# Moving one gate block's weight halves ahead of a plane copy and two turned halves in a two-branch attention kernel

## The chip, the cores and the metric

The kernel runs on one core of a Trainium2 chip. The metric is the device time of one execution in microseconds. Before the change the median of three runs is 749.95 us (749.94 to 751.45). The core has a matrix engine (PE, with its weight loads as PEld), three engines for the rest (DVE, the vector engine; ACT, the scalar engine; POOL, called GpSimd), and SyncE (SP), which here only issues DMAs. Each engine works through its own instructions in the order of the program; between engines there are only semaphore waits.

## The reference, cut to what matters

One layer over 512 frames of width 1024: two attention branches and their gates from one projection, a merge, an output projection, LayerNorm, a gated MLP with a short causal convolution, LayerNorm. Branch A (`dsa`) selects 128 keys per query by top-k over an indexer's scores and then attends with 8 heads of 64; branch B (`sb`) is stick-breaking attention, also 8 heads of 64.

```python
def sb_sequence(q, k, v):                      # per head and block of 128 queries
        causal = s_pos[None, :] < t[:, None]
        z = jnp.einsum('thd,shd->hts', qb, k).astype(jnp.float32) * HEAD_DIM ** -0.5
        log_beta = jax.nn.log_sigmoid(z)
        log_keep = jnp.where(causal, jax.nn.log_sigmoid(-z), 0.0)
        later = lax.cumsum(log_keep, axis=2, reverse=True) - log_keep
        a = jnp.where(causal, jnp.exp(log_beta + later), 0.0).astype(v.dtype)
        return jnp.einsum('hts,shd->thd', a, v)
...
        proj = x @ w_in[layer]
        q_a, k_a, v_a, q_i, k_i, w_i, q_s, k_s, v_s, g_a, g_b = jnp.split(proj, IN_OFFSETS, axis=-1)
...
        y_a = lax.map(lambda a: dsa_sequence(*a, rel_bias),
...
        y_s = lax.map(lambda a: sb_sequence(*a),
...
        gate_a = jax.nn.sigmoid(g_a + b_gates[layer, 0])
        gate_b = jax.nn.sigmoid(g_b + b_gates[layer, 1])
        merged = gate_a * (y_a @ w_branch_dsa[layer]) + gate_b * (y_s @ w_branch_sb[layer])
        x = layer_norm(DEEPNORM_ALPHA * x + merged @ w_out[layer], ln1_g[layer], ln1_b[layer])
        u, g = jnp.split(x @ w_ffn_in[layer], 2, axis=-1)
        h = jax.nn.gelu(causal_dwconv(u, conv_w[layer], conv_b[layer])) * g
        x = layer_norm(DEEPNORM_ALPHA * x + h @ w_ffn_out[layer], ln2_g[layer], ln2_b[layer])
```

## The kernel before, in words

**Arithmetic.** Every f32 operand of a matmul is split into a high half and a low half (rest), each in the matrix engine's fp32r format, and a product is made of three matmuls: high by high, low by high, high by low. In the code the halves of the activations are `xh`, `xl`, those of the weights `whi`, `wlo`. A projection block (`proj_t`, L234 to L236) is 24 matmuls of 512 columns: 8 slices of the width, three products each, into one PSUM bank.

**Weights** stream through `Stream`: a DMA brings a 128x1024 block into `raw` (ring of three), ACT makes the high half `whi` (L105), and the low half `wlo` is made either by DVE or POOL as `raw - whi` (L114) or, for some blocks (the gates gb4 to gb7 among them), by ACT as `-whi` (L108) and a DMA that adds the block from DRAM to it (L111). `asp` says how many blocks ahead the stream splits, `behind` behind which instruction the next high half is tied, `highs` keeps the instruction of L108. The blocks come in a fixed list; around the change it is qa0, ka0, gb4, gb5, gb6, gb7, qa1, ka1, va: the gates of branch B, queries and keys of branch A, its values.

**Heads of branch B.** For one head the scores `z` (L536, PSUM `z_ps`) go through two sigmoids on ACT (L541 `keep`, L542 `beta`), scans on DVE and a product on POOL. The weights are then turned: `send_planes` splits them in two 16-bit planes (L472 on ACT for the high plane `keep<-beta`, L473 on POOL for the low plane) and issues one DMA transpose for each on SP into the single buffer `pl`; `join_planes` puts the planes together again (L483 on ACT, L484 on POOL, into `back`) and splits the result in fp32r halves `pth` (L486, ACT, "turned half") and `ptl` (L491, DVE). `weigh` (L507) multiplies them with the values into `av_ps`, ACT takes one half out (L512, `avt`).

**Around the change** heads 4, 5, 6 and 7 of branch B are under way, one being weighed while the next is turned and the one behind it is scored. Between them stand fillers: gate blocks, then qa1 (copied out by ACT at L357), ka0 and ka1, each taken out of its PSUM bank by `stack_hl` as two ACT copies (L339, L340) and two DVE subtractions (L341, L342), then the values `va` (`proj_v`, L271 to L273), whose four accumulators `va_ps0` to `va_ps3` take the four banks of the same PSUM pool that gb6, gb7, qa1 and ka1 had. DVE also does the rounds of the top-k selection (L424, L425). Behind them the heads of branch A start: logits `l_ps` (L581), masked by DVE (L587, `lg`), exponential on ACT (L590).

**The order.** The program is written in Tile with a scheduler that works out each engine's order from its own estimate of times; the code ties one instruction behind another with `tc.issue_after`. Before the change, head 5's planes are sent as soon as head 5's scans are done (in `advance`), head 4's turned halves follow in `join_planes(..., first=True)`, gb6's high half is tied behind head 4's turned half, and ka0's copies behind gb6's L108. The rounds of selection of turn 4 are tied behind head 4's low half.

Of the kernel before, what the change touches and what calls it, by code (L numbers as in the profile page):

```python
# [49 lines left out]
def r32(ap):  # L50
    return ap.bitcast(F32)
# [77 lines left out]
def tile_block(ctx: ExitStack, tc: tile.TileContext, xT, xN, w_qi, w_ki, w_t, w_v, w_br, w_o, w_fi, w_fo,  # L129
# [305 lines left out]

    firsts, copied, highs_of, joins = [], [], [], {}

    def turned():
        return (bp.tile([128, ATT], F32R, tag="th", bufs=1, name="pth"),
                bp.tile([128, ATT], F32R, tag="tl", bufs=1, name="ptl"))  # L440
# [38 lines left out]
    def join_planes(pl, eng=nc.vector, first=False):  # L479

        back = bp.tile([128, ATT], F32, tag="back", bufs=1, name="back")
        got = pl.rearrange("p a b c -> p a (b c)")
        nc.scalar.activation(halves16(back)[:, 1], got[:, 1], AF.Copy)  # L483
        copied.append(eng.tensor_copy(halves16(back)[:, 0], got[:, 0]).ins)  # L484
        th, tl = turned()
        high = nc.scalar.activation(th, back, AF.Copy).ins  # L486
        highs_of.append(high)
        if first:
            st.behind = high
            firsts.append(high)  # L490
        low = nc.vector.tensor_sub(tl, back, r32(th)).ins  # L491
        if first:
            firsts.append(low)
        h, l = (t.rearrange("p (s c) -> p s c", c=128) for t in (th, tl))
        parts = [(i, o, h[:, c], l[:, c]) for i, o, c in
                 ((0, slice(128, 512), slice(0, 9, 3)), (0, slice(0, 128), slice(2, 3)),
                  (1, slice(128, 512), slice(1, 9, 3)), (2, slice(256, 512), slice(5, 9, 3)),
                  (3, slice(384, 512), slice(9, 10)))]
        return parts
# [122 lines left out]
    def filler(t):  # L622
# [4 lines left out]
        elif kind == "bs":  # L627
            yield from branch(1, "bs", ys, n, use_s)
        else:
            ps = yield from proj_t(t)  # L630
            if kind in ("qs", "qa"):
                qk[t] = stack_dup(ps, 1.0 if kind == "qs" else -0.125, t)
            elif kind in ("ks", "ka"):
                with tc.issue_after(st.highs["gb6"]) if t == "ka0" and firsts else nullcontext():
                    qk[t] = stack_hl(ps, "k", 4, t)
            elif kind == "gb":
                g = xp.tile([128, 512], F32, tag="m", bufs=8, name=t)
                with tc.issue_after(st.highs[f"gb{n+2}"]) if n in (4, 5) else nullcontext():
                    ups[t] = nc.scalar.activation(g, ps, AF.Sigmoid, bias=bgt[:, 8 + n:9 + n]).ins
                m.append(g)  # L640
            elif n >= EARLY:
                gps[n] = ps
            else:
                g = xp.tile([128, 512], F32, tag="y", bufs=12, name=t)
                nc.scalar.activation(g, ps, AF.Identity, bias=bgt[:, n:n + 1])
                early[n] = g
# [59 lines left out]
    def values_of(parts, w, h):  # L706
        if h % 2 == 0:
            pair[w] = bp.tile([128, 512], F32, tag="yt", bufs=2, name=f"y{w}t{h//2}")
        fill_until(f"v{w}")
        ends = weigh(parts, vals[w], h, pair[w])  # L710
        if h % 2 == 1:
            (ys if w == "s" else ya).append(finish_pair(pair[w], f"y{w}{h//2}"))
        return ends
# [1 line left out]
    def advance(i):  # L715
# [6 lines left out]
        last = sb_sticks(*following, {TIED + 1: "gb5", TIED + 2: "gb6"}.get(i))  # L722
        if i < TURN:
            return following[0], last
        return send_planes(*following, nc.gpsimd), last

    pair, joined = {}, None
    for i, (w, h) in enumerate(heads):
        following = start_head(i + 1) if i + 1 < len(heads) else ()
        fill(GAP)  # L730
        ends = ()
        if joined is not None:
# [6 lines left out]
        if w == "s" and i + 1 < H:  # L739
# [16 lines left out]
            with tc.issue_after(following[1]):  # L756
# [2 lines left out]
                        parts = join_planes(weights[0], nc.gpsimd, i == TIED)  # L759
                if i == TIED:  # L760
                    select_some(2)
                    with tc.issue_after(firsts[1]):
                        select_some(ROUNDS[i] - 2)
                else:
                    select_some(ROUNDS[i])
        fill(GAP)
# [542 lines left out]
```

## Time and profile before

| | |
|---|---|
| median of three runs | 749.95 us (749.94 to 751.45) |
| profiled execution | 752.19 us, of it span 750.4 us |
| granted TensorE clock, mean | 0.993 |
| PE busy | 739.1 us (98%) |
| DVE busy | 574.0 us (77%) |
| ACT busy | 408.5 us (54%) |
| POOL busy | 150.3 us (20%) |

The profile is one execution. Its rows give the start of an instruction, its duration, its engine and source line (numbers of the kernel before), output and inputs by the program's names, and in brackets how long the engine stood idle before it and who released it. Matmul rows overlap, so the spacing of starts, not the duration, is what one costs in a row of many. PEclk is the share of full speed that the TensorE clock was granted.

### The profile page before, as it was taken

How to read it: one execution, taken by the hardware profiler on the slowest of the kernel's cores; microseconds unless marked ns; L12 is line 12 of the kernel's file. 1: busy time of each engine (PE TensorE's matmuls, PEld its weight loads, DVE VectorE, ACT ScalarE, POOL GpSimd, SP SyncE). 2: the span in 40 equal slices, each digit the busy share in tenths (PEclk: the TensorE clock that was granted, in tenths of full speed). 3: DMA queues.
4: the chain of work that ended last, by engine and by line, in shares of the span. 5: the costliest groups of instructions: out<-in, count | busy, mean ns of one | idle time of the engine just before them, and what ended most of it. 6: DMA issues, size and time to landing. Idle time of an engine off the chain costs nothing.

```text
span 750.4 us, 9754 instructions
## 1 busy us (share of the span) xinstructions
PE 739.1 (98%) x3477; PEld 619.8 (83%) x3477; DVE 574.0 (77%) x905; ACT 408.5 (54%) x572; POOL 150.3 (20%) x163
## 2 busy tenths in 40 slices
PE   9999999998999999999999999999999999999995
PEld 7888888887888888888889888888888888888885
DVE  5569888999679898568664867676776668668995
ACT  5466867886867588745474533443443344346430
POOL 1002224364733341000011111011101101110011
PEclk9999999998999999999999999999999999999999
DMA  8445887997476554227822444434443434448632
GB/s 271 149 128 191 192 180 168 198 180 180 101 181 166 141 142 116 100 76 225 310 52 68 166 157 154 140 118 164 134 156 130 155 129 147 141 149 281 200 118 84
DMA packets 73631, 117.03 MB, mean 156 GB/s; under 512 B 42536, under 2 KB 42792, under 8 KB 73584
## 3 DMA queue, kind: packets, MB, share of 16 engines
q1 hardware_dynamic: 66304, 93.98, 42.0%
q0 software_dynamic: 5744, 18.38, 9.6%
q10 hardware_dynamic: 1536, 4.06, 2.1%
q8 instruction: 27, 0.44, 0.2%
q14 instruction: 20, 0.16, 0.1%
HBM read 95.93 MB, written 9.98 MB: 141 GB/s over the span
## 4 chain that ended last, share of the span: by engine, by line
PE 94%; DMA 2%; ACT 2%; DVE 1%; issue 0%; ACTq 0%; DVEq 0%; SPq 0%
PE u_ps L949 5%; PE u_ps L947 5%; PE g_ps L949 5%; PE g_ps L947 5%; PE u_ps L948 5%; PE g_ps L948 5%; PE m L1028 2%; PE m L1029 2%; PE m L1027 2%; PE av_ps L507 2%; PE ga_ps L236 2%; PE ga_ps L235 2%; PE ga_ps L234 2%; PE o_ps L877 2%; PE o_ps L876 2%; PE o_ps L878 2%
## 5 line engine op out<-in xcount | busy, mean ns | idle before, releaser
L105 ACT ACTIVATE whi<-raw 128x1024 fp32r<-128x1024 f32 (+1 forms) x124 | 124.0, 1002 | 152.8 <-PE g_ps L948 44.4
L114 DVE TENSOR_TENSOR wlo<-raw,whi 128x1024 fp32r<-128x1024 f32 (+1 forms) x105 | 123.0, 1173 | 39.5 <-ACT whi L105 38.5
L949 PE MATMUL u_ps<-x1h,wlo 128*128 128x512 f32 (+1 forms) x192 | 71.4, 372 | 0.0
L947 PE MATMUL u_ps<-x1h,whi 128*128 128x512 f32 (+1 forms) x192 | 71.3, 372 | 0.0
L948 PE MATMUL u_ps<-x1l,whi 128*128 128x512 f32 (+1 forms) x192 | 71.3, 371 | 0.0
L947 PE MATMUL g_ps<-x1h,whi 128*128 128x512 f32 (+1 forms) x184 | 69.9, 380 | 0.0
L948 PE MATMUL g_ps<-x1l,whi 128*128 128x512 f32 (+1 forms) x184 | 69.9, 380 | 0.0
L949 PE MATMUL g_ps<-x1h,wlo 128*128 128x512 f32 (+1 forms) x184 | 69.9, 380 | 0.0
L948 PEld LDWEIGHTS u_ps<-x1l,whi 128*128 128x128 f32 x192 | 36.2, 188 | 6.3
L949 PEld LDWEIGHTS u_ps<-x1h,wlo 128*128 128x128 f32 x192 | 36.2, 188 | 6.3
L947 PEld LDWEIGHTS u_ps<-x1h,whi 128*128 128x128 f32 x192 | 36.2, 188 | 6.2
L949 PEld LDWEIGHTS g_ps<-x1h,wlo 128*128 128x128 f32 x184 | 34.6, 188 | 6.6
L948 PEld LDWEIGHTS g_ps<-x1l,whi 128*128 128x128 f32 x184 | 34.6, 188 | 6.6
L947 PEld LDWEIGHTS g_ps<-x1h,whi 128*128 128x128 f32 x184 | 34.6, 188 | 6.4
L970 DVE TENSOR_TENSOR t<-raw 128x512 f32<-128x512 f32 x11 | 7.6, 692 | 36.9 <-DMA raw<-in_w_fo_dram 35.5
L570 POOL TENSOR_TENSOR bm<-win,score 128x256 f32<-128x256 f32 (+2 forms) x24 | 26.0, 1107 | 43.0 <-DMA pl<-bm 24.6
L989 POOL MEMSET u<- 128x2 f32 x22 | 2.1, 98 | 146.6 <-ACT whi L105 100.5
L1003 DVE TENSOR_TENSOR hF<-g_ps,c 128x512 f32<-128x512 f32 x22 | 15.1, 687 | 21.0 <-PE g_ps L949 21.0
L995 ACT ACTIVATE c<-c,cwt 128x512 f32<-128x512 f32 x22 | 15.9, 725 | 27.1 <-DVE c L994 26.8
L845 POOL TENSOR_TENSOR rstd<-rstd,mhalf 128x1 f32<-128x1 f32 x8 | 7.7, 958 | 105.0 <-DVE rstd L844 105.0
L424 DVE MAX8 m<-score 128x8 f32<-128x256 f32 (+2 forms) x48 | 26.5, 553 | 1.0 <-DVE score L425 0.2
L551 DVE TENSOR_TENSOR_SCAN keep<-keep,first 128x512 f32<-128x512 f32 (+3 forms) x32 | 27.1, 891 | 0.1
(579 smaller groups left out, 2094.7 us busy)
## 6 DMA issues: line engine op xcount, KB each, us to landing
raw<-in_w_fi_dram SPq DMA_DIRECT2D x44, 512.0 KB, 3.3
raw<-in_w_t_dram SPq DMA_DIRECT2D x32, 512.0 KB, 3.9
raw<-in_w_fo_dram SPq DMA_DIRECT2D x26, 512.0 KB, 3.7
wlo<-in_w_t_dram POOLq DMA_DIRECT2D x14, 512.0 KB, 7.0
raw<-in_w_br_dram SPq DMA_DIRECT2D x8, 512.0 KB, 3.7
raw<-in_w_o_dram SPq DMA_DIRECT2D x8, 512.0 KB, 4.0
raw<-in_w_v_dram SPq DMA_DIRECT2D x7, 512.0 KB, 3.8
raw_b<-in_w_fo_dram SPq DMA_DIRECT2D x6, 512.0 KB, 4.8
```

Of the source, the lines that this page charges most:

```text
L105: self.high = nc.scalar.activation(hi[:, :w], t[:, :w], AF.Copy).ins
L114: self.done[key] = eng.tensor_sub(lo[:, :w], t[:, :w], r32(hi[:, :w])).ins
L234: nc.tensor.matmul(ps[:M], wh[:, c], xh[k], start=(k == 0), stop=False)
L235: nc.tensor.matmul(ps[:M], wh[:, c], xl[k], start=False, stop=False)
L424: nc.vector.max(m8, sc)
L551: scan = nc.vector.tensor_tensor_scan(rev, rev, first[:, 512 - N:512][:, ::-1], 0.0, op0=ALU.mult, op1=ALU.max)
L570: nc.gpsimd.tensor_add(bm[:, OFF[j]:OFF[j] + N], win[:, 512 - N:512], score[j])
L947: nc.tensor.matmul(ps[:, c], wh[:, kc], x1h[:, k, c], start=(k == 0), stop=False)
L948: nc.tensor.matmul(ps[:, c], wh[:, kc], x1l[:, k, c], start=False, stop=False)
L949: nc.tensor.matmul(ps[:, c], wl[:, kc], x1h[:, k, c], start=False, stop=(k == KC - 1))
L995: nc.scalar.activation(c, c, AF.Gelu_apprx_tanh, bias=cwt[:, f, 3:4])
L1003: nc.vector.tensor_mul(F[:, o:o + 2].rearrange("p a b -> p (a b)"), gps_, c)
```

## The change

The join of head 4 no longer makes its halves: it makes `back` and leaves the rest in a closure. `finish_join` makes the halves later, in the filler of ka0, tied behind gb6's L108; ka0's copies are tied behind head 4's high half in place of gb6's L108, and the remaining rounds of selection of turn 4 go there too. In turn 5 the stream splits gb6 first, tied behind head 6's sigmoids, and only then are head 5's planes sent, behind gb6's L108. `asp` is 2 while ka0 is projected and 3 again behind it, so that gb7 is not split earlier.

```diff
--- before.py
+++ after.py
@@ -435,6 +435,15 @@
 
     firsts, copied, highs_of, joins = [], [], [], {}
 
+    waiting = []
+
+    def finish_join():
+        with tc.issue_after(st.highs["gb6"]):
+            parts = waiting.pop()()
+        waiting.append(parts)
+        with tc.issue_after(firsts[1]):
+            select_some(ROUNDS[TIED] - 2)
+
     def turned():
         return (bp.tile([128, ATT], F32R, tag="th", bufs=1, name="pth"),
                 bp.tile([128, ATT], F32R, tag="tl", bufs=1, name="ptl"))
@@ -482,15 +491,16 @@
         got = pl.rearrange("p a b c -> p a (b c)")
         nc.scalar.activation(halves16(back)[:, 1], got[:, 1], AF.Copy)
         copied.append(eng.tensor_copy(halves16(back)[:, 0], got[:, 0]).ins)
+        if first:
+            waiting.append(lambda: halves_of(back))
+            return waiting
+        return halves_of(back)
+
+    def halves_of(back):
         th, tl = turned()
         high = nc.scalar.activation(th, back, AF.Copy).ins
         highs_of.append(high)
-        if first:
-            st.behind = high
-            firsts.append(high)
-        low = nc.vector.tensor_sub(tl, back, r32(th)).ins
-        if first:
-            firsts.append(low)
+        firsts[:] = high, nc.vector.tensor_sub(tl, back, r32(th)).ins
         h, l = (t.rearrange("p (s c) -> p s c", c=128) for t in (th, tl))
         parts = [(i, o, h[:, c], l[:, c]) for i, o, c in
                  ((0, slice(128, 512), slice(0, 9, 3)), (0, slice(0, 128), slice(2, 3)),
@@ -627,11 +637,17 @@
         elif kind == "bs":
             yield from branch(1, "bs", ys, n, use_s)
         else:
+            if t == "ka0":
+                st.asp = 2
             ps = yield from proj_t(t)
             if kind in ("qs", "qa"):
                 qk[t] = stack_dup(ps, 1.0 if kind == "qs" else -0.125, t)
             elif kind in ("ks", "ka"):
-                with tc.issue_after(st.highs["gb6"]) if t == "ka0" and firsts else nullcontext():
+                if t == "ka0":
+                    st.asp = 3
+                    finish_join()
+                    st.behind = firsts[0]
+                with tc.issue_after(firsts[0]) if t == "ka0" else nullcontext():
                     qk[t] = stack_hl(ps, "k", 4, t)
             elif kind == "gb":
                 g = xp.tile([128, 512], F32, tag="m", bufs=8, name=t)
@@ -707,7 +723,7 @@
         if h % 2 == 0:
             pair[w] = bp.tile([128, 512], F32, tag="yt", bufs=2, name=f"y{w}t{h//2}")
         fill_until(f"v{w}")
-        ends = weigh(parts, vals[w], h, pair[w])
+        ends = weigh(parts.pop() if parts is waiting else parts, vals[w], h, pair[w])
         if h % 2 == 1:
             (ys if w == "s" else ya).append(finish_pair(pair[w], f"y{w}{h//2}"))
         return ends
@@ -722,11 +738,18 @@
         last = sb_sticks(*following, {TIED + 1: "gb5", TIED + 2: "gb6"}.get(i))
         if i < TURN:
             return following[0], last
+        if i == TIED + 1:
+            return following, last
         return send_planes(*following, nc.gpsimd), last
 
     pair, joined = {}, None
     for i, (w, h) in enumerate(heads):
         following = start_head(i + 1) if i + 1 < len(heads) else ()
+        if i == TIED + 1:
+            st.asp, st.behind = 3, ups[h + 1]
+            st._advance(st.used)
+            with tc.issue_after(st.highs["gb6"]):
+                weights = send_planes(*weights[0], nc.gpsimd), weights[1]
         fill(GAP)
         ends = ()
         if joined is not None:
@@ -759,8 +782,6 @@
                         parts = join_planes(weights[0], nc.gpsimd, i == TIED)
                 if i == TIED:
                     select_some(2)
-                    with tc.issue_after(firsts[1]):
-                        select_some(ROUNDS[i] - 2)
                 else:
                     select_some(ROUNDS[i])
         fill(GAP)
```

**First place: ACT behind head 6's sigmoids** (`keep<-beta` is head 5's plane copy, `pth<-back` head 4's turned half, `whi_30`, `wlo_30` are gb6, 31 gb7, 32 qa1, `back_1711` is head 5's). Before:

```order
L472 ACTIVATE keep_1500<-beta_1499 128x1280
L486 ACTIVATE pth_1575<-back_1572 128x1280
L105 ACTIVATE whi_30_1617<-raw_30_1615 128x1024
L108 ACTIVATE wlo_30_1618<-whi_30_1617 128x1024
L339 ACTIVATE ka0a_1669<-ka0_ps_1622 64x512
L340 ACTIVATE ka0b_1670<-ka0_ps_1622 64x512
L105 ACTIVATE whi_31_1677<-raw_31_1675 128x1024
L639 ACTIVATE gb4_1748<-gb4_ps_1682,bgt_105 128x512
L108 ACTIVATE wlo_31_1678<-whi_31_1677 128x1024
L483 ACTIVATE back_1711<-pl_1567 128x1280
L105 ACTIVATE whi_32_1752<-raw_32_1750 128x1024
```

Now:

```order
L105 ACTIVATE whi_30_1637<-raw_30_1600 128x1024
L108 ACTIVATE wlo_30_1638<-whi_30_1637 128x1024
L481 ACTIVATE keep_1500<-beta_1499 128x1280
L655 ACTIVATE gb4_1748<-gb4_ps_1682,bgt_105 128x512
L501 ACTIVATE pth_1659<-back_1567 128x1280
L339 ACTIVATE ka0a_1669<-ka0_ps_1602 64x512
L340 ACTIVATE ka0b_1670<-ka0_ps_1602 64x512
L105 ACTIVATE whi_31_1677<-raw_31_1675 128x1024
L108 ACTIVATE wlo_31_1678<-whi_31_1677 128x1024
L492 ACTIVATE back_1711<-pl_1642 128x1280
L105 ACTIVATE whi_32_1752<-raw_32_1750 128x1024
```

gb6's two steps stand ahead of the plane copy; the sigmoid of gb4 and the turned half stand behind it; from `whi_30` to `whi_32` the eleven rows are the same instructions.

**The same place on PE**, from qa1's first two matmuls on (30 is gb6, 31 gb7, 32 qa1). Before:

```order
L234 MATMUL qa1_ps_1923<-xh0_131,whi_32_1752 128x512
L235 MATMUL qa1_ps_1923<-xl0_132,whi_32_1752 128x512
L236 MATMUL gb6_ps_1856<-xh0_131,wlo_30_1618 128x512
L234 MATMUL gb6_ps_1856<-xh1_185,whi_30_1617 128x512
L235 MATMUL gb6_ps_1856<-xl1_186,whi_30_1617 128x512
L236 MATMUL gb6_ps_1856<-xh1_185,wlo_30_1618 128x512
```

Now:

```order
L234 MATMUL qa1_ps_1923<-xh0_131,whi_32_1752 128x512
L235 MATMUL qa1_ps_1923<-xl0_132,whi_32_1752 128x512
L236 MATMUL qa1_ps_1923<-xh0_131,wlo_32_1753 128x512
L234 MATMUL qa1_ps_1923<-xh1_185,whi_32_1752 128x512
L235 MATMUL qa1_ps_1923<-xl1_186,whi_32_1752 128x512
L236 MATMUL qa1_ps_1923<-xh1_185,wlo_32_1753 128x512
```

Behind qa1's first two matmuls now stand qa1's own low half and twenty rows of qa1, and gb6's rest follows those. gb6's first two matmuls have moved from behind head 7's scores to ahead of head 4's weighing.

**Second place: PE where the values begin** (`va_ps0` to `va_ps3` are the value projection's accumulators, `av_ps` the weighing of a head, `l_ps` logits of branch A). Before, `va_ps3` begins after two more slices of the others:

```order
L273 MATMUL va_ps2_2087<-whi_35_1919,xl3_252 128x512
L271 MATMUL va_ps0_2085<-whi_36_2001,xh4_275 128x512
L507 MATMUL av_ps_2110<-pth_2028,vs0_704 128x384
L271 MATMUL va_ps3_2088<-whi_34_1885,xh0_131 128x512
L272 MATMUL va_ps3_2088<-wlo_34_1886,xh0_131 128x512
L273 MATMUL va_ps3_2088<-whi_34_1885,xl0_132 128x512
```

Now, the end of the weighing of head 6 and what follows it (ka1's last matmul stands 15 rows ahead of the first of these):

```order
L517 MATMUL av_ps_1973<-ptl_1833,vs3_713 128x128
L271 MATMUL va_ps2_2087<-whi_34_1885,xh0_131 128x512
L271 MATMUL va_ps3_2088<-whi_34_1885,xh0_131 128x512
L591 MATMUL l_ps_2074<-ka0b_1670,qa0b_1595 128x256 x2
L272 MATMUL va_ps0_2085<-wlo_34_1886,xh0_131 128x512
L273 MATMUL va_ps0_2085<-whi_34_1885,xl0_132 128x512
```

`va_ps3` now begins together with `va_ps2`, 36 rows of PE's program earlier than before, with logits of branch A directly behind it.

DVE at the same place (`ka1a`, `ka1b` are the subtractions that read ka1's bank, `qa1b` reads that of qa1, `lg` are masked logits that read theirs). Before:

```order
L358 SCALAR_TENSOR_TENSOR qa1b_1994<-qa1_ps_1923,qa1b_1994 64x512
L587 ISA lg_1934,mn_1935<-l_ps_1938,bm_1930 128x512
L587 ISA mn_1935 128x1
L594 RECIPROCAL rs_1937<-sm_1936 128x4
L597 TENSOR_SCALAR lg_1934<-lg_1934,rs_1937 128x128
```

Now:

```order
L358 SCALAR_TENSOR_TENSOR qa1b_1994<-qa1_ps_1923,qa1b_1994 64x512
L341 TENSOR_TENSOR ka1a_2079<-ka1_ps_2005,ka1a_2079 64x512
L342 TENSOR_TENSOR ka1b_2080<-ka1_ps_2005,ka1b_2080 64x512
L597 ISA lg_1934,mn_1935<-l_ps_1938,bm_1930 128x512
L597 ISA mn_1935 128x1
```

The two subtractions of ka1 have moved from 11 rows behind the masking of 128x512 logits to directly ahead of it.

## The prediction

> **What bounds the kernel now.** I read the page's busy times first, then PE's waits, then the windows around the one place where the TensorE clock falls.
>
> ```profile
> span 750.4 us, 9754 instructions
> PE 739.1 (98%) x3477; PEld 619.8 (83%) x3477; DVE 574.0 (77%) x905; ACT 408.5 (54%) x572; POOL 150.3 (20%) x163
> ```
>
> PE is busy 98% of the span. No other engine is near it, so the time is PE's matmuls plus what PE stands idle plus what a low clock adds. The view of waits, for PE alone, has the idle part (engine, operation and line waited for: total us, times, longest):
>
> ```profile
> PE qa_ps L234 <- ACT whi L105: 1.6, 1, 1.6
> PE idle_ps L211 <- DVE idle L208: 1.2, 1, 1.2
> PE gb_ps L236 <- DMA wlo<-in_w_t_dram: 1.0, 1, 1.0
> ```
>
> Three waits in 750 us. The middle one is the start of the kernel; the other two stand together, at the change. PE's timeline there (start, us, operation, idle before it and who ended it):
>
> ```profile
> 169.81 0.52 PE L234 MATMUL qa_ps<-xh,whi 128*128 128x512 f32 x1 [1.61 <-ACT whi L105]
> 170.14 0.61 PE L235 MATMUL qa_ps<-xl,whi 128*128 128x512 f32 x1
> 171.73 0.80 PE L236 MATMUL gb_ps<-xh,wlo 128*128 128x512 f32 x1 [0.98 <-DMA wlo<-in_w_t_dram]
> ```
>
> PE wants qa1's high half, which ACT has not made; then gb6's low half, which the adding DMA has not landed. A 512-column matmul, 0.39 us long at other places, goes to 0.6 and 0.8 meanwhile. Windows behind it (us; PE, PEld, DVE, ACT, POOL busy; PEclk is the granted clock; DMA share; GB/s):
>
> ```profile
> 172.00:177.00 5.00, 5.00 (x12) 3.86 (x13) 5.00 (x10) 3.74 (x6) 0.33 (x1) 0.50 0.68 171
> 177.00:180.00 3.00, 3.00 (x15) 2.46 (x14) 2.90 (x7) 0.73 (x1) 2.26 (x2) 1.00 0.74 183
> ```
>
> At clock 0.50 PE does 12 matmuls in 5.00 us without waiting. At full clock one starts every 0.2275 us in the stretch of ka1 (rows below), so the 12 cost 2.73: the low clock loses 2.27 us in 5, or 0.45 per us. The place costs 1.61 + 0.98 idle and about 2.3 of clock.
>
> **The change, first place (168 to 172 us).** No instruction is added or removed; the order on the engines moves. ACT has no gap there:
>
> ```profile
> 158.98 1.31 ACT L472 ACTIVATE keep<-beta 128x1280 uint16<-128x1280 uint16 x1
> 160.14 1.31 ACT L486 ACTIVATE pth<-back 128x1280 fp32r<-128x1280 f32 x1
> 161.30 1.10 ACT L105 ACTIVATE whi<-raw 128x1024 fp32r<-128x1024 f32 x1
> 162.43 1.06 ACT L108 ACTIVATE wlo<-whi 128x1024 fp32r<-128x1024 f32 x1
> ...
> 167.22 1.63 ACT L483 ACTIVATE back<-pl 128x1280 uint16<-128x1280 uint16 x1
> 168.72 1.03 ACT L105 ACTIVATE whi<-raw 128x1024 fp32r<-128x1024 f32 x1
> ```
>
> Ten operations stand from 158.98 to qa1's high half at 168.72, and by the rows of the change the same ten stand there afterwards: only their order differs. Both gb6 steps move to the front (a gain of 161.30 − 158.98 = 2.32 us for gb6), and plane copy and turned half move behind them, but qa1's high half starts at 168.7 as before. **The 1.61 us wait stays.** One thing can make it longer: `back` of head 5 needs head 5's transposed plane, whose copy now starts behind both gb6 steps (1.13 and about 1.0 from start to start) at 161.1 instead of 158.98, and ends at 162.4. The transpose behind it took, in three windows of the view of DMA issues (last number: us from issue to landing), 3.3 us alone, 5.0 with a weight load on its way, 7.2 with a load and an adding DMA beside it:
>
> ```profile
> pl<-keep SPq DMA_TRANSPOSE x1, 3.3
> pl<-keep SPq DMA_TRANSPOSE x1, 5.0
> pl<-keep SPq DMA_TRANSPOSE x1, 7.2
> ```
>
> It now stands behind ka1's weight load and next to gb6's add. It lands between 165.7 and 169.6; `back` wants it at 167.2. I take the middle row, 5.0 us: 167.4, so **+0.2** (bounds 0 and +2.4, the 7.2 us case).
>
> The second wait changes its owner. Behind qa1's first two matmuls PE now wants qa1's low half, which DVE makes by subtraction, and the add of gb6 (in by 171.73 at the latest before, 8.2 us after its negation ended at 163.49; now so counted in by 169.4) is needed only twenty matmuls later. DVE's row for that subtraction, and the page's row for all of them (105, busy us, mean ns):
>
> ```profile
> 170.45 1.93 DVE L114 TENSOR_TENSOR wlo<-raw,whi 128x1024 fp32r<-128x1024 f32 x1
> ```
>
> ```profile
> L114 DVE TENSOR_TENSOR wlo<-raw,whi 128x1024 fp32r<-128x1024 f32 (+1 forms) x105 | 123.0, 1173 | 39.5 <-ACT whi L105 38.5
> ```
>
> qa1's high half ends at about 169.85, so its low half is there at 171.0 to 171.8, against 171.73 before. I take 171.4: **−0.3**, and PE's wait there falls from 0.98 to about 0.7. With the transpose the place nets −0.1 (bounds −0.7 and +2.4). Two waits so close still lower the clock.
>
> What else moves is covered. The transpose of head 5's low plane stands on SP behind va0's weight load, which must wait for gb7's high half (ring of three): some 4 us later. GpSimd's copy into `back` and everything behind it in GpSimd's queue go later with it, but PE reads head 5's weights 14 matmuls later than before, 3.2 us at full clock and twice that in the slow stretch. Without that cover up to 4 − 3.2 = 0.8 us would show. Head 4's turned half is made behind both gb6 steps, the plane copy and a gate's sigmoid, instead of directly behind the plane copy, and DVE, which takes the low half from it, idles that long; on PE two gb6 matmuls now stand ahead of head 4's sums, and the score matmuls of head 7 (`z_ps`) between the high half's first sum and the low half's, so I count it as in time. Without that cover it would show as a wait of L507 for `pth` or `ptl`, up to the 2.3 us that the two gb6 steps take on ACT, less the 0.46 of the two matmuls: 1.9.
>
> **The change, second place (about 200 us).** The scheduler has also moved the value projection's fourth bank, `va_ps3`, 36 rows up in PE's order. It reuses the PSUM bank of ka1, and may begin only when ka1's four copies (L339 to L342, two on ACT and two on DVE) have read it. Before, ka1's last matmul and this one stood far enough apart that it never waited. Now 20 matmuls stand between. I put both sides on the clock of the trace, counting from head 5's last weighing (PE's timeline):
>
> ```profile
> 185.99 0.28 PE L507 MATMUL av_ps<-ptl,vs 128*128 128x128 f32 x1
> ...
> 195.66 0.34 PE L507 MATMUL av_ps<-pth,vs 128*128 128x384 f32 x1
> ...
> 198.91 1.19 PE L581 MATMUL l_ps<-ka0b,qa0b 128*128 128x512 f32 x6
> 199.94 0.85 PE L271 MATMUL va_ps<-whi,xh 128*128 128x512 f32 x3
> ```
>
> *When PE asks.* Before, 36 full matmuls and one group of logits lie between head 5's last and head 6's first weighing, 9.67 us. Afterwards 32 do (4 of gb7, 2 of qa1, 24 of ka1, 2 of va): 9.67 − 4 × 0.2275 = 8.76. Head 6's weighing takes 3.25 us (195.66 to 198.91) with 8 matmuls of ka1 in it, so 1.43 alone; the logits of `l_ps` 1.03; one matmul of va_ps2 0.23. PE asks for va_ps3 at 185.99 + 8.76 + 1.43 + 1.03 + 0.23 = 197.44.
>
> *When the bank is free.* ACT, from head 5's `avt` on:
>
> ```profile
> 186.30 0.59 ACT L512 ACTIVATE avt<-av_ps 64x512 f32<-64x512 f32 x1 [2.10 <-PE av_ps L507]
> ...
> 196.10 0.59 ACT L357 ACTIVATE qa1b<-qa_ps 64x512 fp32r<-64x512 f32 x1
> ...
> 198.19 0.72 ACT L590 ACTIVATE lg<-lg,mn 128x512 f32<-128x512 f32 x1 [1.49 <-DVE mn L587]
> ...
> 199.39 1.05 ACT L105 ACTIVATE whi<-raw 128x1024 fp32r<-128x1024 f32 x1
> 200.46 0.59 ACT L339 ACTIVATE ka1a<-ka_ps 64x512 fp32r<-64x512 f32 x1
> 201.07 0.59 ACT L340 ACTIVATE ka1b<-ka_ps 64x512 fp32r<-64x512 f32 x1
> ```
>
> The stretch from `avt` to the end of qa1b holds the same operations in both orders and no idle time before: 186.30 to 196.69. Then va2's high half (1.07 to the next start), ka1a (0.61) and ka1b (0.59): ACT is through at 198.96. DVE's part follows:
>
> ```profile
> 206.29 0.69 DVE L342 TENSOR_TENSOR ka1b<-ka_ps,ka1b 64x512 fp32r<-64x512 f32 x1
> ...
> 209.36 0.69 DVE L587 CUSTOM_DVE_ANT_0 lg<-l_ps,bm 128x512 f32<-128x512 f32 x1
> ```
>
> With 0.69 and some 0.15 of hand-over, va_ps3 begins at about 199.8: **a new wait of 2.4 us**. Queued behind it on PE are all the other value matmuls. One row later the logits `l_ps` of the next block need their PSUM bank from DVE's masking (L587), which stands behind ka1b's subtraction on DVE: 199.8 + 0.69 + 0.08 = 200.6, where PE is ready at 200.1: **another 0.5**. Bounds of the two together: 0, if ACT is 2.4 us earlier; 4.4, if ACT also loses the 1.49 us that it spent waiting for DVE's masking in the old order.
>
> *Clock.* In the first place 1.61 us of idle were enough for the clock to go to 0.50, until 177.0, 5.3 us behind the second wait. A wait of 2.4 and one of 0.5 a few rows on are alike, so I charge 5 us at 0.45: **+2.3** (bounds 0 and, for 6.9 us, +3.1). [...]
>
> **Sum** against the profiled execution, 752.19 us (750.40 span and 1.79 around it): −0.1 + 2.4 + 0.5 + 2.3 = **+5.1, so 757.3**. That execution is 2.24 above the median of the runs shown, 749.95; I carry the difference over: **755.0**.
>
> **Rivals.**
> - *The new wait is there, the clock stays.* For it: 2.4 us in one place is less idle than 1.61 + 0.98 within 3.6 us. Against: the clock was already down before the 0.98. 749.95 − 0.1 + 2.9 = 752.7. Chance 0.11.
> - *The transpose lands late too* (7.2 us instead of 5.0): +2.2 of wait and +0.3 of clock more, 757.5. For it: an adding DMA and a weight load next to it, as in the 7.2 us row. Chance 0.07.
> - *Nothing comes of it:* ACT reaches ka1's copies in time, and the first place stays as it was; 749.9. It takes an ACT that is 2.4 us earlier against PE than the rows say, as where PE is slow for longer while ACT works on. Chance 0.15.
> - *Faster:* ACT is in time at va_ps3, and the second wait at the first place goes altogether, as DVE's subtraction follows ACT at once and takes the mean 1.17. That saves 0.98 and, if the clock does not see a second wait, one us of it less: 0.98 + 1.5 (3.3 us of slow clock at 0.45) = 2.5, so 747.5. It decides from the point at which ka1's last copy ends ahead of 197.4 and qa1's low half ahead of 170.9. Chance 0.10.
>
> **How the numbers follow.** The forecast, 755.0, has 0.57; the rivals 0.11, 0.07, 0.15 and 0.10. 0.2% of the time (1.5 us) is about what a measurement of this kernel can tell from no change: slower 0.57 + 0.11 + 0.07 = 0.75, same 0.15, faster 0.10. The forecast's own bounds are 752.7 without the clock and 758.5 with ACT's extra 1.5 us and the longer slow stretch (755.0 + 1.5 + 0.8, and something of the transpose). The range goes down to 749.5, which takes in most of "nothing comes of it", and up to 758.5; the faster case and half of the late transpose are left out.
>
> **What would show it.** In the new profile's PE waits: `va_ps` (the L271 of before) waiting for DVE's ka1b, about 2.4 us, and `l_ps` for DVE, about 0.5, both near 200 us; a second stretch of PEclk 0.5 behind them. At the first place the wait for qa1's high half is still 1.6, the wait for the adding DMA is gone, and one of 0.7 or less for DVE's `wlo` stands in its place. I am wrong if no wait of va_ps shows, if the clock stays at 1.0 behind it, or if the first place's waits are gone or have grown past 2 us.

## The result, and the profile after

The changed kernel takes 759.56 us (median of five runs, 758.21 to 761.42) against 749.95 us before (749.58 to 753.38): ratio 1.0119, interval 1.009 to 1.0148. It is slower, as forecast, but by 9.6 us and not by 5.1; the time lies above the stated range.

The profiled execution took 761.42 us. The page's first lines:

```profile
span 759.6 us, 9757 instructions
PE 741.3 (98%) x3477; PEld 620.0 (82%) x3477; DVE 573.4 (75%) x905; ACT 409.7 (54%) x572; POOL 151.8 (20%) x163
```

PE's busy time grew by 2.2 us with the same 3477 matmuls, the span by 9.2. The view of PE's waits has the other part (total us, times, longest):

```profile
PE va_ps L271 <- DVE ka1b L342: 3.6, 1, 3.6
PE qa_ps L234 <- ACT whi L105: 2.4, 1, 2.4
PE idle_ps L211 <- DVE idle L208: 1.2, 1, 1.2
PE av_ps L517 <- DVE ptl L503: 1.1, 2, 0.6
PE av_ps L517 <- ACT pth L501: 0.9, 1, 0.9
PE vs_ps L271 <- ACT whi L105: 0.6, 1, 0.6
PE qa_ps L236 <- DVE wlo L114: 0.5, 1, 0.5
PE gb_ps L236 <- DMA wlo<-in_w_t_dram: 0.4, 1, 0.4
```

Eight rows make 10.7 us where three made 3.8: 6.9 of the 9.2 us are waits, and the other 2.3 are matmuls that take longer. (The 0.6 of `vs_ps` stands at 7 us, at the start of the kernel, far from the change.) The new wait of `va_ps` for ka1b's subtraction is there; the wait for gb6's adding DMA is gone (the row that is left belongs to gb5), and qa1's low half waits 0.5. Behind the two larger waits the clock is down (windows; the third number from the end is the granted clock):

```profile
175.20:178.50 3.30, 3.30 (x9) 2.57 (x8) 3.25 (x8) 3.30 (x8) 3.30 (x2) 0.50 0.69 215
207.40:212.70 5.30, 5.28 (x13) 4.05 (x14) 5.02 (x12) 2.79 (x6) 2.63 (x4) 0.50 0.00 0
```

5.3 us at 0.50 behind va_ps3, 2.4 us lost at the 0.45 per us of the prediction. The first place was slow for 3.3 us, 1.5 us lost, where the profile before lost about 2.3 in 5 us. So the windows place about 1.6 of the 2.3 us; the other 0.7 is not placed. What ended ACT's idle time (start, us, operation, idle before it):

```profile
165.59 1.26 ACT L501 ACTIVATE pth<-back 128x1280 fp32r<-128x1280 f32 x1
...
170.93 1.62 ACT L492 ACTIVATE back<-pl 128x1280 uint16<-128x1280 uint16 x1 [0.82 <-DMA pl<-keep]
172.43 1.03 ACT L105 ACTIVATE whi<-raw 128x1024 fp32r<-128x1024 f32 x1
...
202.07 1.67 ACT L492 ACTIVATE back<-pl 128x1280 uint16<-128x1280 uint16 x1 [1.10 <-DVE ptl L503]
...
205.26 0.59 ACT L340 ACTIVATE ka1b<-ka_ps 64x512 fp32r<-64x512 f32 x1
```

In both places a join (`back`) stands ahead of what PE waits for and waits itself: in the first for head 5's transposed plane, in the second until DVE has read the single `back` buffer of head 6. That reading is slow. DVE, then GpSimd at the same times:

```profile
166.88 2.22 DVE L503 TENSOR_TENSOR ptl<-back,pth 128x1280 fp32r<-128x1280 f32 x1 [1.68 <-ACT pth L501]
...
199.16 2.88 DVE L503 TENSOR_TENSOR ptl<-back,pth 128x1280 fp32r<-128x1280 f32 x1
...
205.89 0.68 DVE L341 TENSOR_TENSOR ka1a<-ka_ps,ka1a 64x512 fp32r<-64x512 f32 x1 [3.12 <-ACT ka1b L340]
206.59 0.69 DVE L342 TENSOR_TENSOR ka1b<-ka_ps,ka1b 64x512 fp32r<-64x512 f32 x1
```

```profile
165.29 2.45 POOL L568 TENSOR_TENSOR beta<-beta,keep 128x1280 f32<-128x1280 f32 x1 [0.16 <-DVE keep L561]
...
198.28 2.41 POOL L114 TENSOR_TENSOR wlo<-raw,whi 128x1024 fp32r<-128x1024 f32 x1
```

In the profile before, head 4's subtraction took 1.46 us with GpSimd idle beside it. Head 6's took 1.49, and there GpSimd began a subtraction 0.01 us behind it:

```profile
162.36 1.46 DVE L491 TENSOR_TENSOR ptl<-back,pth 128x1280 fp32r<-128x1280 f32 x1
...
192.08 1.49 DVE L491 TENSOR_TENSOR ptl<-back,pth 128x1280 fp32r<-128x1280 f32 x1 [3.20 <-ACT pth L486]
```

```profile
192.09 2.64 POOL L520 TENSOR_TENSOR ys2l<-yst,ys2h 128x512 fp32r<-128x512 f32 x1
```

GpSimd's 128x512 subtraction took 1.31 us in the changed kernel, with DVE idle for most of it; here it is the one that is slow.

One more thing is late at the second place. DVE had stood idle for 3.12 us, but both of ka1's subtractions begin behind ACT's second copy, which ended at 205.85: two of them, 0.70 us each, stand between that copy and va_ps3.

### The profile page after: what moved, and what is told of

Read it like the earlier page. It is cut to its first block, busy times and chain, and to the rows that moved or that the text cites. A ratio compares the mean times of both kernels' runs of the same rounds, so it can differ in the third digit from the quotient of the medians.

```text
span 759.6 us, 9757 instructions
## 1 busy us (share of the span) xinstructions
PE 741.3 (98%) x3477; PEld 620.0 (82%) x3477; DVE 573.4 (75%) x905; ACT 409.7 (54%) x572; POOL 151.8 (20%) x163
## 4 chain that ended last, share of the span: by engine, by line
PE 91%; ACT 3%; DMA 3%; DVE 2%; issue 1%; SPq 0%; POOL 0%; DVEq 0%; ACTq 0%
PE u_ps L968 5%; PE u_ps L969 5%; PE g_ps L968 5%; PE u_ps L970 5%; PE g_ps L969 5%; PE g_ps L970 5%; PE m L1050 2%; PE m L1048 2%; PE m L1049 2%; PE av_ps L517 2%; DMA pl<-keep 2%; PE ga_ps L236 2%; PE ga_ps L235 2%; PE ga_ps L234 2%; PE o_ps L899 2%; PE o_ps L898 2%
```

## The experiments

All diffs are against the changed kernel where nothing else is said; medians stand beside the median of the kernel before, run along with them. Theory A was at first: the wait at the values, with the clock behind it, is the larger part; the first place lost by lateness on ACT.

**The changed kernel, profiled again.** No edit.

> The changed kernel, profiled a second time. In the first profile head 4's low plane took 9.7 us to land (7.2 before the change), which started ACT's whole chain about 2.5 us later. If that is how one execution differs from another, this profile has a landing near 7 us, ACT's gb6 high half near 159.5 instead of 161.76, no waits of the weighing for head 4's halves, and about 2 us less in all (758 to 760). If the change itself makes it late, it is again above 9 us. The wait of va_ps3 for ka1's copies is there in both cases, 2.4 to 3.6 us, with clock 0.5 behind it.

759.48 us (one run). PE's waits behind the start:

```profile
PE va_ps L271 <- DVE ka1b L342: 3.6, 1, 3.6
PE qa_ps L234 <- ACT whi L105: 3.2, 1, 3.2
...
PE av_ps L517 <- DVE ptl L503: 0.6, 1, 0.6
PE av_ps L517 <- ACT pth L501: 0.2, 1, 0.2
```

Head 4's low plane landed after 8.3 us (9.7 in the first profile, 7.2 before the change), gb6's high half started at 159.78, and the waits for head 4's halves shrank to 0.2 and 0.6. But qa1 waited 3.2 us, as `back` waited 1.61 for head 5's plane, and va_ps3 3.6 again. So head 4's late halves were partly one execution's luck; the other two waits belong to the order. The clock was low for 6.8 us at the first place and 3.4 at the second, the other way round than in the first profile (3.4 and 6.8).

**va_ps3 sixteen rows later on PE.**

```diff
-            if which == "va" and g == 3:
+            if which == "va" and g in (0, 3):
                 steps.sort(key=lambda t: t[1])
...
-                nc.tensor.matmul(pss[i], xh[k][:, r], wh[:, c], start=(k == 0), stop=False)
+                with tc.issue_after(third) if (which, k, i) == ("va", 0, 3) else nullcontext():
+                    nc.tensor.matmul(pss[i], xh[k][:, r], wh[:, c], start=(k == 0), stop=False)
...
-                nc.tensor.matmul(pss[i], xl[k][:, r], wh[:, c], start=False, stop=(k == KC - 1))
+                third = nc.tensor.matmul(pss[i], xl[k][:, r], wh[:, c], start=False, stop=(k == KC - 1)).ins
```

> The changed kernel with va_ps3's first matmul put 16 rows later on PE (behind the first two slices of the other three banks), ACT and DVE as they are. Theory A (the wait comes from the chain of ACT and DVE behind ka1, on which the logits' bank hangs as well): va_ps3's wait goes, but the logits of 128x256, which stand ahead of it now, wait for DVE's masking behind ka1's subtractions, 3.5 to 4.5 us: no gain, 758.5 to 760.5. Theory B (only ka1's bank was in the way): 4 to 6 us less, 754 to 756.

759.05 us (758.47 to 760.55) against 750.67: ratio 1.0115 (1.0094 to 1.0137), no gain. PE's first waits now:

```profile
PE l_ps L592 <- DVE mn L598: 4.3, 1, 4.3
PE qa_ps L234 <- DVE score L426: 2.4, 1, 2.4
```

(The second row names DVE's selection; qa1's high half on ACT ended at 171.26, and PE began at 171.31.) The wait moved whole to the logits, whose bank hangs on a masking that stands behind ka1's subtractions on DVE. PE's order was not the cause; the chain ACT to DVE was late for everybody.

**ka1's copies first.** The second place's chain shortened where it is late: ka1's two ACT copies stand ahead of va2's high half and of head 7's join.

```diff
-            if t == "ka0":
+            if t in ("ka0", "ka1"):
                 st.asp = 2
...
+                if t == "ka1":
+                    st.asp = 3
+                    st.behind = stacked[-1]
...
+                    if w == "s":
+                        fill_until("ka1")
                     with ExitStack() as ties:
-                        for ins in (emptied["va"] if (w, h) == ("a", 1) else ()) + (following[1], ups[(h + 1) % H]):
+                        for ins in (emptied["va"] if (w, h) == ("a", 1) else ()) + (following[1], ups[(h + 1) % H]) + ((stacked[-1],) if w == "s" else ()):
```

(`stacked` holds the second ACT copy of each `stack_hl`.)

> The changed kernel with ka1's two ACT copies directly behind the logits' exponential, ahead of va2's high half and of head 7's join. Theory A (the second place, a wait of 3.6 us for ka1's copies plus about 2.4 us of low clock, is the larger part of the loss): the copies end some 3 us earlier, the wait shrinks to 0.6 or less plus at most 0.6 for the logits, no low clock behind it: 754 to 755, some 5 us less than the changed kernel. Theory B (PE loses the time at the first place, and the second only takes up what would be waited for later): at most 1.5 us less, 758 or more.

756.95 us (754.19 to 758.43) against 750.67: ratio 1.0079 (1.0053 to 1.0105), 2.6 us less than the changed kernel, about half of what was expected and more than theory B allowed. The waits of the profiled run, its fastest (754.19):

```profile
PE qa_ps L234 <- DVE score L425: 2.3, 1, 2.3
PE av_ps L517 <- ACT pth L501: 1.4, 1, 1.4
...
PE va_ps L271 <- DVE ka1b L342: 0.5, 1, 0.5
PE qa_ps L236 <- DVE wlo L114: 0.5, 1, 0.5
PE l_ps L591 <- DVE mn L597: 0.2, 1, 0.2
```

(The first row stands for qa1's high half again.) The wait at the values went from 3.6 to 0.7, as reckoned, and the clock stays at 1.0 there. A new one of 1.4 us came 8 us later: head 7's turned half is late for its own weighing. ACT had joined its high plane by 201.6, but DVE's copy of the low plane stood behind the scalings of the logits:

```profile
206.02 0.90 DVE L493 COPY back<-pl 128x1280 uint16<-128x1280 uint16 x1
```

The first place is as it was.

**Head 5's plane copy ahead of gb6 again**, the swap that the change is named for, undone. PE, DVE, GpSimd and SP keep their order.

```diff
-        if i == TIED + 1:
-            return following, last
         return send_planes(*following, nc.gpsimd), last
...
-            st.asp, st.behind = 3, ups[h + 1]
+            st.asp, st.behind = 3, highs_of[-1]
             st._advance(st.used)
-            with tc.issue_after(st.highs["gb6"]):
-                weights = send_planes(*weights[0], nc.gpsimd), weights[1]
```

> The changed kernel with one swap undone: head 5's plane copy stands ahead of gb6's two steps on ACT again, all other orders are the same. Theory A (the named swap costs little; the loss is in the second place and in head 4's late halves): head 5's planes land about 2 us earlier, ACT's wait for them (0.8 us) goes, qa1's high half comes 0.8 us earlier: 758 to 759.5, 0 to 1 us less than the changed kernel. Theory B (the swap that the change is named for is what costs): back to 750 to 752.

761.7 us (759.25 to 764.74) against 750.67: ratio 1.0149 (1.0112 to 1.0185). Both theories missed: undoing the swap gained nothing. Two of the four runs (759.25, 759.69) lie among the changed kernel's, two (763.72, 764.74) above all of them, so whether it costs anything stays open. ACT's join and SP's queue in the profiled run, the slowest, show why nothing is gained:

```profile
168.71 1.63 ACT L492 ACTIVATE back<-pl 128x1280 uint16<-128x1280 uint16 x1 [2.01 <-DMA pl<-keep]
```

```profile
160.64 0.33 SPq L74 DMA_DIRECT2D raw<-in_w_t_dram  x1
161.15 1.68 SPq L484 DMA_TRANSPOSE pl<-keep  x1
```

The copy ended at 159.7, but the transpose left at 161.15: on SP it still stood behind ka1's weight load, which waits until gb6's high half, now later, has read its `raw` buffer. It then landed after 7.5 us. Here the early copy was worth nothing, as the queue behind it had not moved with it.

**qa1 ahead of the join.** gb5 is projected before head 5's join is placed, so that qa1's high half stands ahead of `back` on ACT. gb6 and all else that the change moved stay; the scheduler puts va_ps3 17 rows later, behind ka1's copies.

```diff
                 if not turns and not ahead:
+                    if i == TIED + 1:
+                        fill_until("gb5")
                     with tc.issue_after(ups[h + 1]), tc.issue_after(st.high):
```

> The changed kernel with the same addition (qa1's high half ahead of head 5's join). va_ps3 comes 17 rows later. Theory A (the changed kernel loses because its new order makes late transposes and ka1's copies fall on the path, not by gb6's place): the wait for the transposed plane no longer stands ahead of qa1, no wait of 2 us or more at the values: 749 to 754. Theory B (late head 4 halves alone cost most): 756 or more.

749.19 us (747.85 to 752.11, ten runs) against 750.37: ratio 0.9989 (0.9975 to 1.0003). Ten us come back at once, with gb6 still ahead of plane and halves. PE's waits:

```profile
PE qa_ps L236 <- DVE wlo L114: 1.1, 1, 1.1
PE l_ps L591 <- DVE ka2a L341: 0.4, 1, 0.4
PE va_ps L271 <- DVE ka1b L342: 0.3, 1, 0.3
PE qa_ps L234 <- DVE ka0b L342: 0.2, 1, 0.2
```

(The row of the kernel's start is left out.) In this profile the clock is 1.00 in every window from 166 to 216 us; its mean is 0.997 to 0.998 in all ten runs, against 0.989 to 0.991 in the changed kernel's five. At the first place head 5's join now begins at 177.86, behind head 7's sigmoids; at the second, head 7's join stands behind ka1's copies, and head 6's `ptl` takes 1.72 in place of 2.88.

**The same edit in the kernel before.**

> The kernel before with one change: gb5 is projected before head 5's join is placed, so that qa1's high half stands ahead of the join on ACT (and its low half is used ahead of gb6's on PE); head 5's planes, head 4's halves and gb6 stay where they were. Theory A (the wait of 1.6 us and the low clock behind it come from ACT's 1.5 us of join ahead of qa1): qa1's wait goes to 0.2 or less, one of about 1 us for DVE's low half stays, possibly no low clock: 745 to 749. Theory B (the time reappears at head 5's weighing or at ka1's copies, as in the changed kernel): 750 to 757.

753.03 us (751.8 to 755.77) against 750.37: ratio 1.0036 (1.002 to 1.0052). qa1's own wait went to 0.2, but its low half waited longer than both of the old waits together, and head 6's half (the 1.4) came late:

```profile
PE qa_ps L236 <- DVE wlo L114: 3.4, 1, 3.4
PE av_ps L507 <- ACT pth L486: 1.4, 1, 1.4
```

In this order GpSimd's copies of planes ran beside the subtraction, and it took 2.65 us (its row on DVE):

```profile
169.31 2.65 DVE L114 TENSOR_TENSOR wlo<-raw,whi 128x1024 fp32r<-128x1024 f32 x1
```

That is 1.4 us more than the 1.23 of other places. As much again came from DVE's queue: the high half was there at 167.84, and a round of selection stood ahead of the subtraction until 169.31.

Whether gb6's early place itself makes the edit pay in the changed kernel, or only the order that the scheduler finds around it, these two runs don't tell.

**Head 4's halves ahead of the plane copy.**

```diff
             with tc.issue_after(st.highs["gb6"]):
+                finish_join()
+            with tc.issue_after(st.highs["gb6"]), tc.issue_after(firsts[0]):
                 weights = send_planes(*weights[0], nc.gpsimd), weights[1]
```

(The call in the filler of ka0 goes.)

> The changed kernel with head 4's turned halves moved one place up, ahead of head 5's plane copy (both still behind gb6's two steps). The scheduler then puts head 5's join behind qa1's high half, and va_ps3 19 rows later on PE, behind ka1's copies. Theory A (late head 4 halves and a late qa1 high half make the first place, the wait on ka1's copies the second): waits for pth gone, qa1's wait under 1 us, no wait of 2 us or more at the values: 747 to 752. Theory B (gb6 ahead of the turned halves costs by itself, whatever the order behind it): 755 or more.

753.28 us (751.28 to 756.57) against 750.37: ratio 1.0038 (1.0022 to 1.0054), between the theories. The scheduler again put qa1's high half ahead of the join and va_ps3 behind ka1's copies, and the waits for qa1's high half and for va_ps3 went (one of 0.9 us for ka0's bank is in the place of the first). Head 4's half was in time, its low half was not: DVE's `ptl` took 3.39 us beside GpSimd's product, everything behind it on DVE came late, and PE waited 3.0 us for qa1's low half.

**Only GpSimd moved.** Head 6's product stands behind gb7's adding DMA, so that GpSimd is idle while DVE makes head 4's low half. It is the one swap; no other engine's order changes.

```diff
-        last = sb_sticks(*following, {TIED + 1: "gb5", TIED + 2: "gb6"}.get(i))
+        last = sb_sticks(*following, {TIED + 1: "gb5", TIED + 2: "gb7"}.get(i))
```

> The changed kernel with one swap on GpSimd: the product of head 6 (128x1280) stands behind gb7's adding DMA, so that GpSimd stands idle while DVE makes head 4's low half. Theory A (DVE's subtraction is slow because GpSimd runs beside it): head 4's ptl takes 1.46 to 1.5 us in place of 2.2 to 2.3, PE's wait for it (0.5 to 0.6) goes; the wait of 3.6 us at the values stays: 757.5 to 759. Theory B (it is slow for another reason, its place behind ACT's late half): ptl stays at 2.2 or more, no change, 759 to 760.

759.28 us (758.26 to 759.72) against 750.94, no change in time. The subtraction answered as theory A had it, and PE no longer waits for it:

```profile
163.84 1.49 DVE L503 TENSOR_TENSOR ptl<-back,pth 128x1280 fp32r<-128x1280 f32 x1 [1.53 <-ACT pth L501]
```

PE came earlier to qa1 and waited 2.7 us there in place of 2.4: ACT's chain ends last at this place, and what DVE gains is handed on to it.

**Selection behind qa1's low half.** The edit that brought ten us back, and the rounds of selection tied behind head 4's low half put behind qa1's low half.

```diff
-        with tc.issue_after(firsts[1]):
-            select_some(ROUNDS[TIED] - 2)
...
+                    if i == TIED + 1:
+                        fill_until("gb5")
+                        with tc.issue_after(st.done["qa1"]):
+                            select_some(ROUNDS[TIED] - 2)
```

> The changed kernel with qa1's high half ahead of head 5's join, and two rounds of the selection put behind qa1's low half on DVE. Theory A (PE's last wait at the first place, 1.1 us for qa1's low half, is DVE's queue of selection work): the wait falls to 0.5 or less, 748 to 749.2, 0.5 us or so less than without the move. Theory B (the low half waits for its high half on ACT, or the selection is late behind it): no gain, 749 to 751.

749.0 us (747.67 to 753.01, twelve runs) against 750.94: ratio 0.9979 (0.9963 to 0.9994). This beats both kernels, by 0.2% over the kernel before. Over the join alone (ratio 0.9989, 0.9975 to 1.0003) no gain is shown, as the two intervals overlap; but the wait for qa1's low half fell from 1.1 to 0.5, as theory A had it. PE's waits behind the start:

```profile
PE av_ps L515 <- DVE ptl L501: 0.5, 1, 0.5
PE qa_ps L236 <- DVE wlo L114: 0.5, 1, 0.5
PE l_ps L589 <- DVE ka2a L341: 0.4, 1, 0.4
```

**And head 6's product later, too.**

> The same with head 6's product behind gb7's adding DMA as well, so that GpSimd is idle beside DVE's head 4 low half. Theory A (DVE at full speed there gives the rest of the wait back): head 4's ptl 1.47 in place of 2.27, PE waits for neither ptl nor qa1's low half for more than 0.4 us, 747.5 to 749. Theory B (the delayed product makes head 6 late): a wait of the weighing for head 6's halves, 750 or more.

752.63 us (751.15 to 755.34) against 750.94: ratio 1.0025 (1.0013 to 1.0036), 3.6 us more than without. Both theories missed the reason; DVE and GpSimd have it:

```profile
165.93 1.49 DVE L501 TENSOR_TENSOR ptl<-back,pth 128x1280 fp32r<-128x1280 f32 x1 [1.66 <-ACT pth L499]
170.13 3.75 DVE L114 TENSOR_TENSOR wlo<-raw,whi 128x1024 fp32r<-128x1024 f32 x1 [1.29 <-ACT whi L105]
```

```profile
170.01 2.78 POOL L566 TENSOR_TENSOR beta<-beta,keep 128x1280 f32<-128x1280 f32 x1
```

The product no longer slows head 4's low half (1.49), but now runs beside qa1's low half, which takes 3.75 us in place of 1.23, and PE waits 3.1 us for it.

**The kernel before, profiled again.** No edit.

> The kernel before, profiled a second time: what changes from one execution to another. Head 4's low plane lands 6.5 to 8.5 us after its issue, the two waits are 1.5 to 3.5 us together with a low clock of 5 us behind them, and ptl (128x1280 on DVE) takes 1.46 to 1.49 us for heads 4 to 6, where the changed order has shown 2.2 to 3.3 for heads 4 and 6. 749 to 752.

750.31 us. Its waits, and the window behind the first:

```profile
PE qa_ps L234 <- ACT whi L105: 1.5, 1, 1.5
...
PE vs_ps L271 <- ACT whi L105: 1.0, 1, 1.0
PE va_ps L271 <- DVE ka1b L342: 0.7, 1, 0.7
```

```profile
170.00:172.00 2.00, 1.66 (x6) 1.16 (x7) 1.97 (x3) 2.00 (x5) 1.82 (x2) 1.00 1.06 317
```

This time gb6's DMA was in time, and the clock stayed at 1.00 behind a wait of 1.5 us, as it did behind the 0.7 us of `va_ps` (`vs_ps` is the start of the kernel again; the mean clock is 0.998). So `va_ps` can wait for ka1 in the old order too, for 0.7 us. Head 6's `ptl`, begun at 191.55, took 1.68 and not 1.49 at most, with GpSimd busy for all of the 4 us from 190 to 194.

## Why the prediction was wrong, step by step

**What bounds it, and the new wait: right.** PE stays the bound, the rows of waits are those named (va_ps3 for ka1b, qa1's low half in place of gb6's DMA), and the second stretch of clock 0.50 is there: behind the wait 5.3 us of it in the profile and 3.0 in the second, where 5 were charged. One of the prediction's own signs of being wrong shows as well: the wait for qa1's high half grew past 2 us.

**Where the 4.1 us are.** From profile to profile the sum was +5.1 and the measured step +9.2. The terms, forecast against measured: the first place −0.1 and +2.2, the waits at the values +2.9 and +4.2, the clock and all else in the matmuls +2.3 and +2.3. The wait at the start of the kernel, +0.6, is in no term and differs from execution to execution.

**The step that failed first is the first place, −0.1, with its "what else moves is covered": +2.2** (4.8 us of waits, gb5's DMA with them, against 2.6). The transpose was costed with the row of 5.0 us; it took 5.7 in the profile and 6.4 in the second one and made `back` wait 0.8 and 1.6 us where 0.2 was charged, and qa1's wait grew by as much. That is within the stated bounds, but the middle row was the wrong choice: 5.7 to 6.4 is what it took in the five profiles of this order in which `back` waited for it. And head 4's halves, counted "as in time", cost 1.5 us in the profile and 0.7 in the second. Of that, the 0.6 of the low half comes from a subtraction of 2.2 us beside GpSimd's product where the old row has 1.46: with the product moved away, it took 1.49 and PE did not wait for it. The other covers held: no wait for head 5 shows. (One reading is off without harm: by its row qa1's high half ended at 169.75, not 169.85.)

**The term for the values, +2.9 of waits, was too small: 4.2** (3.6 for va_ps3, 0.6 for head 6's `ptl`). Two steps failed. DVE's part behind ACT's last copy was charged as one subtraction, 0.69 and 0.15; it was two and took 1.58 from the end of that copy (205.85) to va_ps3's start (207.43), in both profiles alike: 0.7 too little. And ACT did not run from head 5's `avt` to ka1's copies without idle time. It waited 1.10 us (0.58 in the second profile) for DVE to release `back`, as DVE's subtraction, 1.49 in the profile before, took 2.88 (2.35). PE waited for that subtraction too, so not all of ACT's delay comes on top. (The 0.5 for the logits was hidden under the larger wait; with va_ps3 moved away it appeared there, with the rest.)

**The clock term, +2.3, had the right size, in part by luck.** The place it was charged to lost 2.4 us in the profile and about 1.3 in the second; the first place, counted as unchanged, lost about 0.8 less than before in the profile. A wait of 1.61 us was "enough" in one profile; 1.51 us was not in the next. The 3.3 us of slow clock in the faster rival were the author's estimate, with no row behind them; stretches of 3.4 us showed afterwards.

**"I carry the difference over" came out by luck.** It cost only 0.4 us, as the changed kernel's profile lies 1.86 us above its median, near the 2.24 of before. But the reasons differ. In the 24 runs of the kernel before that stand beside the join experiment, the eleven with a mean clock of 0.996 or more took 749.28 to 750.53, the thirteen with less 750.27 to 753.53; the profile, at 0.993, is of the second kind, with a low clock at the first place that the second profile of before doesn't have. The changed kernel's first profile has its late plane instead. Between the two second profiles, each within 0.1 us of its median, the span also grew by 9.2 us, and there it is 4.4 of waits and about 4.3 of low clock (some 9.5 us of it behind PE's waits, at 0.45). Read so, the low clock at the first place is a cost of the change, and the sum had it in the base.

**The range.** The bounds of the three terms (2.4, 4.4 and 3.1) add up to +9.9, which holds the measured +9.6. The range stopped at 758.5, which takes in much of the second and third and little of the first. The first two came near their ends together.

**What the join experiment settles, and what it doesn't.** gb6's place alone does not cost the ten us: with gb6 there and qa1 ahead of the join they are gone. In the changed kernel a join stands on ACT ahead of what PE waits for at both places, and waits itself; in the join experiment neither does, and the waits and the low clock go. That the two joins are the whole cause is argued, not shown: the scheduler moved va_ps3, head 5's join and more with them, and in the kernel before the same edit cost 2.7 us. The shares of the two places outside the profile stay open: shortening the second alone gave 2.6 us of median (with a new wait of 1.4).

## What to carry to other kernels

When a change reorders several engines, list what will run beside each step on the path, not only what stands ahead of it in its own queue: here DVE's subtractions took 1.5 and 1.9 times what the old trace had, once GpSimd had begun beside them. Count every step that stands behind the last one of another engine: two subtractions, not one, stood behind ACT's copy. Take a second profile of the kernel before: what differs between the two (here 1.9 us, with a low clock in one of them) is not a fixed base for a sum. And before a step is moved to feed the path, ask what already stands directly ahead of the path's next step: one join moved out of the way gave back ten us in the changed kernel, though in the kernel before the same move cost 2.7.

## What the runs showed of the hardware

- **DVE beside GpSimd.** The subtraction of 128x1280 f32 took 1.46 to 1.49 us with GpSimd idle and 2.2 to 3.4 beside one of its 128x1280 products or 128x1024 subtractions; the 128x1024 one 1.20 to 1.23 and up to 3.75. The growth is in the instruction's own time, not in a wait for another engine. Moving the product alone took the first from 2.22 to 1.49; with qa1 ahead of the join it then landed beside the second and took that from 1.23 to 3.75. Beside these products and subtractions the one that began second was the one that grew, by nearly what was left of the other: with 0.86, 1.53 and 2.04 us of GpSimd's work left, the 128x1280 subtraction took 2.22, 2.88 and 3.39 us. Where DVE began first, by 0.01 us, it kept its 1.49, and GpSimd's 128x512 subtraction went from 1.31 to 2.64. Why they slow each other was not shown; the prediction did not weigh that they do.
- **The clock.** It fell to 0.50 at a single wait of PE of 1.61 us (the profile before) and at every one of 2.3 to 4.3 us in eight profiles; it stayed at 1.00 behind 1.51 (the second profile of before), 1.40 (ka1's copies first), 1.1 (qa1 ahead of the join) and 0.7. What decides it was not tried. The low stretches at the two places lasted 3.4 us or 6.8: 6.8 at the first place of the profile before, 3.4 and 6.8 in the changed kernel's first profile, 6.8 and 3.4 in its second. At 0.45 us per us that makes 1.5 or 3.1 us, less what falls into the wait itself. So several short waits in different places can be cheaper than one long one: the second profile of before had 3.2 us in three waits and a mean clock of 0.998, while 2.9 in one place (2.3 and 0.5) cost a stretch of 3.4 with ka1's copies first.
- **Landing times.** The same DMA transpose of head 4's low plane took 6.5 to 9.7 us in the eleven profiles whose view of DMA issues has it alone. In the changed kernel the sigmoids that start ACT's chain waited for it, 2.74 us behind a landing of 9.7 and 1.03 behind one of 8.3; with an issue 0.5 us later in the first case, gb6's high half started at 161.76 against 159.78, 2 us apart.
